# Gated one-hots on VectorE: one bf16 compare over eight tokens and wide fp32 multiplies in place of fused fp32 tensor_scalars

## The chip, the cores and the metric
The kernel runs on one core of a Trainium2 chip. The metric is the device time of one execution in microseconds; three timed runs of the kernel before gave a median of 1782.91 us (1781.59 to 1785.38 us). One further execution was recorded by the hardware profiler and is read below.

## The reference, cut to what matters
The program is one step of a decoder layer for 576 tokens (512 of a prompt, 64 of samples): windowed attention and a spatial gating unit in parallel, a merge, then a retrieval over 128 x 128 single-neuron experts (PEER), then a small per-layer gate. The change touches the retrieval alone. In the reference, for each token and each of 8 heads, 16 experts are chosen, and their outputs are added with a weight:

```
cand = (s_top[:, :, 0, :, None] + s_top[:, :, 1, None, :]).reshape(blk, PEER_HEADS, -1)
best, pos = lax.top_k(cand, PEER_TOPK)
idx = jnp.take_along_axis(cand_idx, pos, axis=-1)      # e0 * 128 + e1
gate = jax.nn.softmax(best, axis=-1)
act = jax.nn.gelu(jnp.einsum('thkd,td->thk', expert_u[idx], xb))
out = jnp.einsum('thkd,thk->td', expert_v[idx], gate * act)
```

A token thus has 128 chosen experts (8 heads x 16), each with a first index e0, a second index e1 and a gate.

## The kernel before, in words
The kernel computes the retrieval in two ways. For 192 tokens it gathers the chosen rows of the two expert tables from memory, one row per token by an indirect DMA on GpSimd's queue (line 707), and VectorE takes a dot product with each row (line 719) or adds it with its weight (line 726). For the other 384 tokens it computes all 16384 experts densely: stage 1 (function `stage1`, line 761 on) multiplies the tokens by 128 blocks of the first table, stage 2 (line 939) by 128 blocks of the second, and between the two the activations are multiplied by a gate plane (line 974) that is zero where an expert was not chosen.

Each weight block of either stage is loaded by SyncE's queue and split on the chip in two parts: ScalarE rounds it (w_hi, line 66) and VectorE subtracts (w_lo, line 67), and TensorE runs three products in place of one (line 82).

The gate planes are built by `build_g`, once for each of 24 groups of 16 tokens, in four steps of four tokens. For one token, the 128 chosen experts lie on the partitions. One one-hot matrix (128 x 128, expert by index) is made from e0, another from e1, one of the two carries the gate, and a matmul of the two (line 822) gives the 128 x 128 gate plane of the token. Transposed indices and gates for 128 tokens stand in a tile `ew` (columns: minus the gate, e1, the gate, e0), made by `make_ew` on ScalarE.

The four steps of a group alternate. In the even ones ScalarE makes the gated one-hot `oa` of e0, eight instructions for four tokens (lines 810 and 811), and VectorE the plain one-hot `ob` of e1, one compare of 512 elements a partition (line 813). In the odd ones VectorE makes both: the plain `oa` by one compare of 512 (line 816), and the gated `ob` by four instructions, each of which compares and multiplies one token's 128 elements (line 819). ScalarE then evicts the four planes to the tile `gs` (line 823), reading them across so that the four tokens lie side by side, and SyncE's queue writes `gs` to memory once per group.

The groups are not alone. The loop over `tb` runs some blocks of stage 1 ahead of each group up to a goal, the rest of the expert retrieval (lines 611 to 693) between the first groups, and `pay` lets a few gathers through per block and per group (none from group 22 on). VectorE therefore holds, in one queue, the one-hots, the splits of the weights, the retrieval and the dot products of the gathered rows; `rowp` has 5 row buffers, so GpSimd's next gather waits for VectorE. The order of the instructions on each engine is fixed before the run by the framework's scheduler, from priorities and its own estimates of cost.

Of the kernel before, what the change touches and what calls it, by code (L numbers as in the profile page):

```python
# [9 lines left out]
BF16 = mybir.dt.bfloat16  # L10
U32 = mybir.dt.uint32
AF = mybir.ActivationFunctionType
ALU = mybir.AluOpType
# [4 lines left out]
P = 128  # L18
# [6 lines left out]
TB = 16  # L25
# [3 lines left out]
SPILL = set(range(2, 40, 2))  # L29
NSP = len(SPILL)  # L30
GT = (2.0, 3.5)
ONE = (1, 2)
TAIL0 = 112
TAIL1 = 122
S1_TOPK = (4, 9, 13)
# [12 lines left out]
def tile_decoder_step(ctx: ExitStack, tc: tile.TileContext, a, o):  # L48
    nc = tc.nc
    V, A, T, G, S = nc.vector, nc.scalar, nc.tensor, nc.gpsimd, nc.sync  # L50

    def pool(stack, name, bufs, side="left", **kw):
        return stack.enter_context(tc.tile_pool(name=name, bufs=bufs, side=side, reuse_waits="tile", **kw))
# [6 lines left out]
    def cload(name, shape, pl=None):  # L60
        t = (pl or const).tile(shape, F32, name="c_" + name, bufs=1)
        S.dma_start(t, a[name])
        return t
# [62 lines left out]
    def bank(tag):  # L126
        return psB.tile([P, 512], F32, name=tag)
# [50 lines left out]
    for k in range(KC):  # L178
        with tc.high_priority(offset=500):
# [3 lines left out]
                               op0=ALU.mult, op1=ALU.subtract)  # L183
# [22 lines left out]
    iota = cload("iota", [P, P])  # L206
# [251 lines left out]
    for i in range(24):  # L458
        if i < 8:
            t, g = (svT, suT)[i // 4], i % 4  # L460
            z = t[:, g, :]
            w_chunk(6 + i, z, lambda cols: A.activation(z[:, cols], z[:, cols], AF.Gelu_apprx_tanh))
        else:
            c, br = divmod(i - 8, 2)
# [63 lines left out]
    for c0, r in tilesA:  # L528
# [4 lines left out]
        for hh in range(2):  # L533
            hs = slice(hh * 512, (hh + 1) * 512)
            pt = bank("pt")
            for k in range(4):
                x1k = x1[hh * 4 + k][:, c0:c0 + r]
                T.transpose(out=pt[:r, k * P:(k + 1) * P], in_=x1k, identity=ident)
                if r == NS:
# [3 lines left out]
                                   op0=ALU.mult, op1=ALU.mult)  # L543
# [186 lines left out]
    for i in range(16):  # L730
        h, c = i // 4 + i % 2 * 4, i // 2 % 2
# [14 lines left out]
    ewT = []  # L746
# [35 lines left out]
    def make_ew(e0, e1_, gtf):  # L782
        pt = bank("pt")
        for q, src in enumerate((e1_, gtf, e0)):
            T.transpose(out=pt[:, q * P:(q + 1) * P], in_=src, identity=ident)
        ew = ep.tile([P, 4, P], F32, name="ew")
        A.activation(ew[:, 1:4, :], pt[:, 0:3 * P].rearrange("p (a b) -> p a b", a=3), AF.Copy)
        A.activation(ew[:, 0, :], pt[:, P:2 * P], AF.Copy, scale=-1.0)
        ewT.append(ew)

    found = {}
    tqs.close()
# [1 line left out]
    gs_s = ExitStack()  # L794
    ep = pool(gs_s, "ep", 2)
    op = pool(gs_s, "op", 2)
    gsp = [pool(gs_s, "gsp%d" % i, 1) for i in range(2)]

    def build_g(tb):
        ti, t0 = divmod(tb * TB, P)  # L800
        ew = ewT[ti]
        gs = gsp[(tb + 1) % 2].tile([P, NJ, TB], F32, name="gs")
        for t4 in range(0, TB, 4):
            pt = psB.tile([P, 512], F32, name=("sc", "pt")[t4 // 4 % 2])
            oa = op.tile([P, 4, P], F32, name="oa")
            ob = op.tile([P, 4, P], F32, name="ob")
            c = t0 + t4
            if (tb * TB + t4) // 4 % ONE[1] < ONE[0]:
                for t in range(4):
                    A.activation(oa[:, t, :], iota, AF.Abs, scale=-1.0, bias=ew[:, 3, c + t:c + t + 1])  # L810
                    A.activation(oa[:, t, :], oa[:, t, :], AF.Relu, scale=ew[:, 0, c + t:c + t + 1],
                                 bias=ew[:, 2, c + t:c + t + 1])
                V.tensor_tensor(ob, iota[:, None, :].to_broadcast([P, 4, P]),
                                ew[:, 1, c:c + 4][:, :, None].to_broadcast([P, 4, P]), op=ALU.is_equal)
            else:
                V.tensor_tensor(oa, iota[:, None, :].to_broadcast([P, 4, P]),
                                ew[:, 3, c:c + 4][:, :, None].to_broadcast([P, 4, P]), op=ALU.is_equal)
                for t in range(4):
                    V.tensor_scalar(ob[:, t, :], iota, ew[:, 1, c + t:c + t + 1], ew[:, 2, c + t:c + t + 1],
                                    op0=ALU.is_equal, op1=ALU.mult)  # L820
            for t in range(4):
                T.matmul(pt[:, t * P:(t + 1) * P], lhsT=oa[:, t, :], rhs=ob[:, t, :], start=True, stop=True)  # L822
            A.activation(gs[:, :, t4:t4 + 4], pt.rearrange("p (t j) -> p j t", t=4), AF.Copy)
        if tb == NB // TB - 1:
            A.activation(g0, gs[:, 0:JB, :], AF.Copy)
        S.dma_start(gd[:, :, tb].rearrange("c p j t -> p c (j t)"), gs.rearrange("p (c j) t -> p c (j t)", j=JB))
# [11 lines left out]
    for tb in range(NB // TB):  # L838
        if tb == TBK:
            for i, r_ in enumerate(rest_t):  # L840
                for _ in r_:
                    pass
                make_ew(*found[5 - len(rest_t) + i])
            tks.close()
            late = pool(aLs, "aL", 1, "right")
            acp.append(late.tile([P, RING - NXP, NB], F32, name="aL"))
            g0 = late.tile([P, JB, TB], F32, name="g0")
        if tb < TBK:
            goal = S1_TOPK[2] + (tb + 1) * (S1_PRE - S1_TOPK[2]) // TBK
        else:  # L850
            goal = S1_PRE + (tb - TBK + 1) * (NSP + RING - 1 - S1_END - S1_PRE) // (NB // TB - TBK)
        while len(acts) < goal:
            stage1()
        if tb == 0:
            make_ew(*found[2])
        build_g(tb)
        for _ in range(2):
            if rest_t and next(rest_t[0], 1) == 1:
                rest_t.pop(0)
                make_ew(*found[4 - len(rest_t)])  # L860
        pay(GT[tb >= TBK] if tb < 22 else 0)
# [267 lines left out]
```

## Time and profile before
| | |
|---|---|
| median of three timed runs | 1782.91 us |
| profiled execution | 1776.88 us |
| its span, first to last instruction | 1775.1 us |
| TensorE, VectorE, ScalarE busy | 98%, 81%, 49% |
| stretch in which the gate planes are built | 605 to 882 us |
| granted TensorE clock, mean | 0.996 of full speed |

A busy TensorE is modelled from pipelined matmuls, so a busy share near full may still hide gaps; the pitch of undisturbed matmuls shows how many. The durations of VectorE's instructions overlap by some 0.08 us, so what one of them costs its queue is read from its start to the start of the next.

### The profile page before, as it was taken

To read this page: it belongs to the slowest core of one execution; us is meant where nothing else is said; L and a number is where in the kernel's file an instruction comes from. 1 tells how busy PE (TensorE), PEld (TensorE's weight loads), DVE (VectorE), ACT (ScalarE), POOL (GpSimd) and SP (SyncE) were. 2 spreads that over 40 slices of the span, in tenths; PEclk is the share of its full clock that TensorE was granted. 3 is DMA by queue.
4 is the path that set the end of the run, shared out by engine and by line. 5 is a ranking of instruction groups with operands and counts; after the bars stand their busy time and mean duration, and the time that the engine had idled before them with its cause. 6 is when DMAs were issued, how large, how long until landed. Compare 5 with 4: busy or idle time off the path is not lost.

```text
span 1775.1 us, 27763 instructions
## 1 busy us (share of the span) xinstructions
PE 1744.3 (98%) x10094; PEld 1575.1 (89%) x10094; DVE 1434.0 (81%) x2876; ACT 867.0 (49%) x1525; POOL 525.9 (30%) x390
## 2 busy tenths in 40 slices
PE   7999999999999899999999999999999999999998
PEld 7988999999999899999988887899899899887876
DVE  6455556548999999999898888998888888999862
ACT  6567444343236698999833333333333333333441
POOL 0000000000002112455245554454544554566300
PEclk9999999999999999999999999999999999999999
DMA  7211233443226577999999999999999999999741
GB/s 242 75 60 38 71 105 122 141 152 106 81 92 225 173 244 235 361 350 355 352 388 367 371 388 364 394 410 369 365 338 360 364 334 331 335 379 376 284 132 70
DMA packets 176457, 457.06 MB, mean 257 GB/s; under 512 B 15552, under 2 KB 76736, under 8 KB 174272
## 3 DMA queue, kind: packets, MB, share of 16 engines
q1 hardware_dynamic: 120736, 253.22, 40.6%
q0 software_dynamic: 55584, 202.07, 30.8%
q8 instruction: 79, 1.29, 0.3%
q14 instruction: 58, 0.48, 0.1%
HBM read 420.18 MB, written 35.78 MB: 257 GB/s over the span
## 4 chain that ended last, share of the span: by engine, by line
PE 77%; issue 7%; DVE 6%; DMA 5%; POOL 3%; ACT 1%; SPq 0%; DVEq 0%; POOLq 0%; ACTq 0%
PE mm L82 36%; PE oacc L939 21%; PE pv L82 5%; POOL row L707 3%; PE sc L822 2%; DMA row<-peer_v,idx 2%; PE pt L822 2%; PE oacc L902 2%; DVE w_lo L67 2%; PE sc L82 1%; DMA x1c<-ad 1%; DVE row L719 1%; DMA row<-peer_u,idx 1%; PE sc L580 1%; PE pv L447 1%
## 5 line engine op out<-in xcount | busy, mean ns | idle before, releaser
L66 ACT ACTIVATE w_hi<-w_raw 128x1024 fp32r<-128x1024 f32 x325 | 343.9, 1059 | 372.9 <-PE mm L82 287.1
L707 POOL DMA_INDIRECT row<-peer_u,idx x192 | 261.1, 1360 | 872.0 <-issue 520.8
L67 DVE TENSOR_TENSOR w_lo<-w_raw,w_hi 128x1024 fp32r<-128x1024 f32 x325 | 396.6, 1221 | 74.0 <-ACT w_hi L66 73.7
L82 PE MATMUL mm<-xd,w_hi 128*128 128x384 f32 x1552 | 405.9, 341 | 0.5 <-ACT w_hi L66 0.5
L82 PE MATMUL mm<-x,w_hi 128*128 128x256 f32 (+1 forms) x1600 | 329.7, 300 | 9.8 <-ACT x L181 9.5
L707 POOL DMA_INDIRECT row<-peer_v,idx x192 | 263.3, 1372 | 231.8 <-DVE acc L726 202.8
L82 PEld LDWEIGHTS mm<-xd,w_hi 128*128 128x128 f32 x1552 | 281.6, 189 | 5.9 <-ACT w_hi L66 0.8
L82 PEld LDWEIGHTS mm<-x,w_hi 128*128 128x128 f32 x1600 | 257.8, 190 | 24.1 <-ACT x L181 10.0
L82 PE MATMUL mm<-xd,w_lo 128*128 128x384 f32 x776 | 264.4, 341 | 3.7 <-DVE w_lo L67 3.7
L726 DVE SCALAR_TENSOR_TENSOR acc<-row,wts,acc 128x1024 f32<-128x1024 f32 x192 | 245.8, 1280 | 5.3 <-DMA row<-peer_v,idx 4.9
L939 PE MATMUL oacc<-w_hi,wl 128*128 128x512 f32 x768 | 242.0, 397 | 3.7 <-DVE wl L67 3.6
L939 PE MATMUL oacc<-w_lo,wh 128*128 128x512 f32 x768 | 242.0, 396 | 0.4 <-DVE w_lo L67 0.4
L939 PE MATMUL oacc<-w_hi,wh 128*128 128x512 f32 x768 | 242.3, 396 | 0.0
L719 DVE SCALAR_TENSOR_TENSOR row<-row,xr 128x1024 f32<-128x1024 f32 x192 | 231.6, 1221 | 11.0 <-DMA row<-peer_u,idx 8.6
L82 PE MATMUL mm<-x,w_lo 128*128 128x256 f32 (+1 forms) x800 | 236.6, 296 | 0.0
L939 PEld LDWEIGHTS oacc<-w_hi,wl 128*128 128x128 f32 x768 | 144.3, 188 | 39.6 <-DVE wl L67 5.5
L939 PEld LDWEIGHTS oacc<-w_lo,wh 128*128 128x128 f32 x768 | 144.4, 188 | 35.5 <-DVE w_lo L67 1.7
L939 PEld LDWEIGHTS oacc<-w_hi,wh 128*128 128x128 f32 x768 | 143.7, 188 | 29.4 <-ACT xr L921 0.8
L82 PEld LDWEIGHTS mm<-x,w_lo 128*128 128x128 f32 x800 | 151.7, 190 | 1.1 <-issue 0.8
L82 PEld LDWEIGHTS mm<-xd,w_lo 128*128 128x128 f32 x776 | 147.0, 189 | 4.7 <-DVE w_lo L67 4.7
L82 PE MATMUL pv<-xd,w_hi 128*128 128x384 f32 x496 | 136.7, 348 | 0.7 <-ACT x L776 0.7
L66 ACT ACTIVATE wh<-x 128x384 fp32r<-128x384 f32 x66 | 34.7, 526 | 162.6 <-PE oacc L939 153.1
(304 smaller groups left out, 2308.8 us busy)
## 6 DMA issues: line engine op xcount, KB each, us to landing
w_raw<-peer_uT SPq DMA_DIRECT2D x128, 512.0 KB
w_raw<-peer_v SPq DMA_DIRECT2D x128, 512.0 KB
gd<-gs SPq DMA_DIRECT2D x24, 1024.0 KB
gs<-gd SPq DMA_DIRECT2D x15, 1536.0 KB
w_raw<-w_in SPq DMA_DIRECT2D x30, 512.0 KB
w_raw<-peer_wq SPq DMA_DIRECT2D x16, 512.0 KB
w_raw<-w_br SPq DMA_DIRECT2D x8, 512.0 KB
w_raw<-w_out SPq DMA_DIRECT2D x8, 512.0 KB
```

What stands on the lines that cost most here:

```text
L66: A.activation(hi, src, AF.Copy)
L67: V.tensor_sub(lo, src, hi.bitcast(F32))
L82: mark_pe[0] = T.matmul(ps, lhsT=w[wi][:, wk + k, :], rhs=x[xi][k], start=i == 0, stop=i == n - 1)
L447: T.matmul(ps[:r], lhsT=xi[:, k, :r], rhs=wl_[k][wi][:, hh * 512:(hh + 1) * 512], start=i == 0, stop=i == 5)
L580: T.matmul(ps[:, b * P:(b + 1) * P], lhsT=qp[:, b * P:(b + 1) * P], rhs=sk, start=True, stop=True)
L707: ins = G.indirect_dma_start(out=row_, out_offset=None, in_=table, in_offset=bass.IndirectOffsetOnAxis(ap=ix, axis=0))
L719: V.scalar_tensor_tensor(row_, row_, 1.0, xrs[ti], op0=ALU.mult, op1=ALU.mult, accum_out=dots[:, s:s + 1])
L726: V.scalar_tensor_tensor(accs[ti], row_, wts[:, s:s + 1], accs[ti], op0=ALU.mult, op1=ALU.add)
L822: T.matmul(pt[:, t * P:(t + 1) * P], lhsT=oa[:, t, :], rhs=ob[:, t, :], start=True, stop=True)
L902: T.matmul(ps[hh][:r], lhsT=xi[:, k, :r], rhs=w[k][wi][:, hh * 512:(hh + 1) * 512], start=k == 0 and xi is xh and wi == 0, stop=k == KC - ...
L939: mark_pe[0] = T.matmul(oacc[t][hh], lhsT=wi[:, ts], rhs=vi[:, hh * 512:(hh + 1) * 512], start=j == 0 and last == 0 and vi is vh, stop=j = ...
```

## The change: what it does
The odd steps of a group change on VectorE. Before the four steps, one tensor_tensor compares, for the eight tokens of the two odd steps, a bf16 copy of the index ramp (`iota4`, each index repeated for four tokens, made once on ScalarE) with a bf16 copy of e1 (`ewh`, cast by ScalarE in `make_ew`). Its result `hot` is bf16 and holds, for each index, two runs of four tokens. In each odd step one tensor_tensor then multiplies `hot`, read so that the index runs innermost, by the fp32 gate and writes `ob` in fp32 as before. The four fused tensor_scalars of the step are gone. `hot` has one buffer; the new tiles lie in a pool of their own (`hp`). The even steps, `oa`, the matmuls and the evictions stay. The pattern that picked the odd steps (`ONE`) is written out and picks the same ones.

```
+        ewh = ep.tile([P, P], BF16, name="ewh")
+        A.activation(ewh, pt[:, 0:P], AF.Copy)
...
+    hp = pool(gs_s, "hp", 1)
+    iota4 = hp.tile([P, P, 4], BF16, name="iota4")
+    A.activation(iota4, iota[:, :, None].to_broadcast([P, P, 4]), AF.Copy)
...
+        hot = hp.tile([P, P, 2, 4], BF16, name="hot")
+        e1c = ewh[:, t0:t0 + TB].rearrange("p (g s t) -> p g s t", g=2, s=2)[:, :, 1, :]
+        V.tensor_tensor(hot, iota4[:, :, None, :].to_broadcast([P, P, 2, 4]),
+                        e1c[:, None].to_broadcast([P, P, 2, 4]), op=ALU.is_equal)
...
-                for t in range(4):
-                    V.tensor_scalar(ob[:, t, :], iota, ew[:, 1, c + t:c + t + 1], ew[:, 2, c + t:c + t + 1],
-                                    op0=ALU.is_equal, op1=ALU.mult)
+                V.tensor_tensor(ob, hot[:, :, t4 // 8, :].rearrange("p x t -> p t x"),
+                                ew[:, 2, c:c + 4][:, :, None].to_broadcast([P, 4, P]), op=ALU.mult)
```

## Rows read from the trace of the kernel before

**Rows 1.** Engine totals of the page: busy us, share of the span, instructions.
```profile
PE 1744.3 (98%) x10094; PEld 1575.1 (89%) x10094; DVE 1434.0 (81%) x2876; ACT 867.0 (49%) x1525; POOL 525.9 (30%) x390
```

**Rows 2.** Busy time of each engine by stretch: us, busy (instructions), clock, DMA.
```profile
605.00:720.00 115.00, 112.63 (x722) 108.47 (x723) 113.44 (x308) 104.67 (x227) 24.10 (x17) 0.99 0.77 240
720.00:840.00 120.00, 119.85 (x800) 114.80 (x799) 119.05 (x236) 111.97 (x270) 61.06 (x41) 1.00 1.04 358
840.00:882.00 42.00, 42.00 (x280) 39.88 (x279) 34.87 (x63) 38.11 (x92) 11.16 (x9) 1.00 0.99 353
...
882.00:1140.00 258.00, 251.31 (x1189) 216.15 (x1188) 228.85 (x297) 89.34 (x121) 128.31 (x92) 1.00 0.98 379
```

**Rows 3.** Chain of waits: 605 to 720 and 720 to 840 us by line; two pieces.
```profile
by line: PE pv L82 29.6%; PE mm L82 21.8%; PE pt L822 12.2%; PE sc L822 12.0%; DVE row L719 3.1%; DVE w_lo L67 3.0%; DVE ob L819 2.6%; issue 1.9%; DVE oa L816 1.6%; ACT sp L632 1.6%; DVE c L625 1.3%; DVE pos L627 1.2%; PE pt L785 1.2%; DVE 
by line: PE pv L82 31.6%; PE mm L82 30.2%; PE sc L822 19.0%; PE pt L822 17.9%; issue 0.7%; DVE ob L813 0.5%; DVE row L719 0.1%; DVEq L67 0.0%
...
737.96 0.90 PE pt L822 x8
...
753.33 4.16 PE mm L82 x24
```

**Rows 4.** The same stretches, of one line's instructions: L82, L822, then VectorE's L813.
```profile
720.00:840.00 120.00, 91.44 (x435) 73.86 (x436) 1.00 1.04 358
...
720.00:840.00 120.00, 53.82 (x365) 47.44 (x363) 1.00 1.04 358
...
605.00:720.00 115.00, 12.35 (x18) 0.99 0.77 240
720.00:840.00 120.00, 15.21 (x23) 1.00 1.04 358
840.00:882.00 42.00, 5.46 (x8) 1.00 0.99 353
```

**Rows 5.** Waits of TensorE's weight loads, 605 to 882 us: total, times, longest.
```profile
PEld sc L822 <- ACT oa L811: 4.6, 17, 1.0
PEld pt L785 <- DVE e L658: 3.6, 1, 3.6
...
PEld pt L822 <- DVE ob L819: 0.2, 1, 0.2
```

**Rows 6.** Groups of VectorE instructions, 605 to 882 us: count, busy us, mean ns.
```profile
L819 DVE TENSOR_SCALAR ob<-c_iota,ew 128x128 f32<-128x128 f32 x192 | 55.2, 349 | 0.1
L67 DVE TENSOR_TENSOR w_lo<-w_raw,w_hi 128x1024 fp32r<-128x1024 f32 x43 | 52.5, 1222 | 4.7 <-ACT w_hi L66 4.6
...
L813 DVE TENSOR_TENSOR ob<-c_iota,ew 128x512 f32<-128x512 f32 x48 | 33.0, 688 | 2.1 <-PE sc L822 1.1 <-PE pt L822 0.8
...
L653 DVE TENSOR_TENSOR l<-pr 128x1024 bf16<-128x1024 bf16 x6 | 4.1, 690 | 0.0
```

**Rows 7.** VectorE in order of time: start us, us, instruction.
```profile
639.70 0.70 DVE L653 TENSOR_TENSOR l<-pr 128x1024 bf16<-128x1024 bf16 x1
640.30 0.22 DVE L682 RECIPROCAL den<-den 128x8 f32<-128x8 f32 x1
...
734.86 1.22 DVE L67 TENSOR_TENSOR w_lo<-w_raw,w_hi 128x1024 fp32r<-128x1024 f32 x1
735.99 0.69 DVE L813 TENSOR_TENSOR ob<-c_iota,ew 128x512 f32<-128x512 f32 x1
736.60 0.69 DVE L816 TENSOR_TENSOR oa<-c_iota,ew 128x512 f32<-128x512 f32 x1
737.20 1.11 DVE L819 TENSOR_SCALAR ob<-c_iota,ew 128x128 f32<-128x128 f32 x4
738.23 0.68 DVE L813 TENSOR_TENSOR ob<-c_iota,ew 128x512 f32<-128x512 f32 x1
```

**Rows 8.** Groups of ScalarE's evictions of 512 elements: count, busy us, mean ns.
```profile
L823 ACT ACTIVATE gs<-pt 128x512 f32<-128x512 f32 x48 | 28.2, 587 | 1.2 <-PE pt L822 0.9
...
L451 ACT ACTIVATE st<-pv 128x512 f32<-128x512 f32 x8 | 4.7, 588 | 6.7 <-PE pv L447 6.7
```

More of the change, by code (lines that the diff above doesn't have):

```diff
@@ L31 @@
 GT = (2.0, 3.5)
-ONE = (1, 2)
 TAIL0 = 112
@@ L786, in make_ew @@
         ew = ep.tile([P, 4, P], F32, name="ew")
+        ewh = ep.tile([P, P], BF16, name="ewh")
+        A.activation(ewh, pt[:, 0:P], AF.Copy)
         A.activation(ew[:, 1:4, :], pt[:, 0:3 * P].rearrange("p (a b) -> p a b", a=3), AF.Copy)
         A.activation(ew[:, 0, :], pt[:, P:2 * P], AF.Copy, scale=-1.0)
-        ewT.append(ew)
+        ewT.append((ew, ewh))
     found = {}
@@ L797, in tile_decoder_step @@
     gsp = [pool(gs_s, "gsp%d" % i, 1) for i in range(2)]
+    hp = pool(gs_s, "hp", 1)
+    iota4 = hp.tile([P, P, 4], BF16, name="iota4")
+    A.activation(iota4, iota[:, :, None].to_broadcast([P, P, 4]), AF.Copy)
     def build_g(tb):
         ti, t0 = divmod(tb * TB, P)
-        ew = ewT[ti]
+        ew, ewh = ewT[ti]
+        hot = hp.tile([P, P, 2, 4], BF16, name="hot")
+        e1c = ewh[:, t0:t0 + TB].rearrange("p (g s t) -> p g s t", g=2, s=2)[:, :, 1, :]
+        V.tensor_tensor(hot, iota4[:, :, None, :].to_broadcast([P, P, 2, 4]),
+                        e1c[:, None].to_broadcast([P, P, 2, 4]), op=ALU.is_equal)
         gs = gsp[(tb + 1) % 2].tile([P, NJ, TB], F32, name="gs")
@@ L807, in build_g @@
             c = t0 + t4
-            if (tb * TB + t4) // 4 % ONE[1] < ONE[0]:
+            if t4 // 4 % 2 == 0:
                 for t in range(4):
```

## The prediction
> **What bounds the kernel now.** I read the page's engine totals first [rows 1]: TensorE is busy 1744.3 us of a span of 1775.1 us, VectorE 1434.0 us. The totals say "TensorE", but they average over stages, and the change lives in one stage only, the building of the gate planes from 605 to 882 us. So the second view is the table by stretches of that stage [rows 2]. In it three engines are nearly full at once: from 605 to 720 us TensorE is busy 112.63 and VectorE 113.44 of 115 us, from 720 to 840 us 119.85 and 119.05 of 120 us, and ScalarE 104.67 and 111.97 us. Only from 840 to 882 us, where no gathers are paid for any more, does VectorE have room (34.87 of 42 us).
>
> Two full engines don't tell which one paces. The chain of waits does [rows 3]: from 605 to 720 us VectorE's rows (row L719, w_lo L67, ob L819, oa L816, c L625, pos L627) hold 3.1 + 3.0 + 2.6 + 1.6 + 1.3 + 1.2 = 12.8% of it beside TensorE; from 720 to 840 us the chain is TensorE for 98.7% and VectorE's ob for 0.5%. A busy TensorE is modelled, so I check it by its pitch: 24 matmuls of 384 columns run in 4.16 us when nothing holds them (0.173 us each) and 8 of the fp32 gate matmuls in 0.90 us (0.1125 us each) [rows 3]. With the counts of 720 to 840 us [rows 4] that is 435 x 0.173 + 365 x 0.1125 = 75.3 + 41.1 = 116.4 of 120 us: TensorE can win at most 3.6 us there, whatever VectorE does. What it does wait for in the stage is mostly not the changed code: 4.6 us for ScalarE's oa (L811), 3.6 us for the retrieval's e (L658) [rows 5].
>
> **The change part by part.** Durations overlap from one VectorE instruction to the next, so I price by the slot, from one start to the next start [rows 6, 7].
> Removed, in each group of 16 tokens: two sets of four tensor_scalars. Their rows say 349 ns each, but a set that starts at 737.20 lets the next instruction start at 738.23: 1.03 us a set, 2.06 us a group.
> Added, per group: one bf16 compare of 1024 elements a partition, and two multiplies of 512 elements.
> The compare: all three operands are bf16, and the innermost run in each is four tokens. The retrieval's bf16 tensor_tensor of the same size (L653) takes 690 ns, where the fp32 subtraction of 1024 takes 1222 ns [rows 6]; one that starts at 639.70 is followed at 640.30, a slot of 0.60 us [rows 7]. From above it is bounded by the slot of the fp32 form, 734.86 to 735.99, 1.13 us. I take 0.60, since L653 has the same types and halves down to short runs.
> The multiplies: 512 elements, fp32 gate, fp32 result, so the nearest row is the fp32 compare of 512 (L813, 688 ns), slot 735.99 to 736.60, 0.61 us. That is the lower end. But their first operand is read across: the four-token block is turned, so neighbouring elements of the inner run lie eight bf16, 16 bytes, apart. No VectorE row reads like that. The upper end is the slot of a pass twice as long, 1.13 us for 1024 elements. The nearest row for reading across is ScalarE's eviction of the gate planes, which picks its inner four elements 512 bytes apart and takes 587 ns, against 588 ns for a straight eviction of 512 elements (L451) [rows 8]: no loss. It is another engine and another memory, but it is the only access of this kind in the trace, and I take 0.61 and keep 1.13.
> Sum: 2.06 - (0.60 + 2 x 0.61) = 0.24 us less of VectorE per group, 5.8 us for 24 groups.
>
> The Trainium skill speaks against the multiplies. "SBUF — State Buffer" (Door 1, the note on cachelines) has 16-byte lines and wants at least two hits on a line for full rate; an inner step of 16 bytes hits each line once. The same note counts eight bf16 as a free stride, so it can be read both ways; the trace has no VectorE row to decide. By the strict reading the sum would be that of the first rival below.
>
> What of 5.8 us reaches the end? The compares on line 813 begin 18 times before 720 us, two a group, so 9 groups lie in the stretch where VectorE is on the chain, 23 starts or 11.5 groups lie in 720 to 840 us, and 4 groups behind it [rows 4]. In the first stretch 9 x 0.24 = 2.2 us can move the chain; as TensorE holds most of that chain too, I take 2.0. In 720 to 840 us the saving (2.8 us) becomes VectorE idle time behind a TensorE that paces, and in 840 to 882 us it joins the idle time that is there.
> Moved: the compare stands ahead of a group's first ob. It waits for the last multiply of the group before (one buffer), on the same engine, so nothing new is waited for; what queues behind it is the group's first ob for 0.60 us, inside a VectorE queue that gets shorter on the whole. In a VectorE-gated group the first gate matmul now waits for a whole multiply (0.61 us) where it waited for one tensor_scalar, and the fourth stops waiting 0.4 us earlier; TensorE issues them in a row of four and has other matmuls between, so I cost it at nothing. Should that cover fail, it is at most 0.35 us x 48 groups of four = 17 us, but TensorE waited for ob L819 for 0.2 us in the whole stage [rows 5], and so I don't count it.
> ScalarE gets three casts of 128 elements and one fill of 512, each no larger than what takes 0.59 us in rows 8, so under 2.4 us together. The fill and the first cast come before the first group; the other two casts stand ahead of evictions that a later group needs, and these casts are the only part on ScalarE's path, under 1.2 us in a stage in which it has 22 us free [rows 2]. No DMA is added or moved. Behind 882 us nothing is touched; the DMA share there is 0.98 [rows 2], and a start earlier by 2 us may be given back in part, which the range holds.
>
> So the profiled execution, 1776.88 us (its span and 1.78 us around it), would be 1774.9. The median of the three timed runs is 1782.91, 6.0 us above the profiled one; on that scale I forecast 1780.9 us. A change of 0.2%, 3.6 us, is about what a measurement of this kernel can tell from none, and the forecast lies inside.
>
> **Rivals.**
> 1. The turned read costs double, slower. If each multiply holds VectorE for 1.13 us, a group gains 2 x 0.52 - 0.24 = 0.80 us. VectorE has 1.6 us free in 605 to 720 and 1.0 us in 720 to 840 us: 9 x 0.80 - 1.6 = 5.6, and 11.5 x 0.80 - 1.0 = 8.2, while the last four groups fit in the idle 7 us. Together +13.8, 1796.7 us. It decides from the point where a multiply's slot exceeds about 0.79 us (two multiplies then eat the saving and the idle 2.6 us over 20.5 groups). For it: no VectorE row shows a read across, and VectorE has no room to hide one. Against it: ScalarE's turned read at full rate [rows 8]. The Trainium skill's note on cachelines, in its strict reading, is for it.
> 2. VectorE paces all the way to 840 us. Then 20.5 x 0.24 = 4.9 us come off, 1778.0 us. For it: VectorE is busy 119.05 of 120 us and the gathers wait for its rows; against it: the chain's 98.7% of TensorE.
> 3. The bf16 compare doesn't run at the fast rate with runs of four and repeated operands: 1.13 us instead of 0.60, +0.29 us a group, 9 x 0.29 - 1.6 = 1.0 and 11.5 x 0.29 - 1.0 = 2.3, so +3.3, 1786.2 us. Against it: L653's 690 ns.
> 4. It does nothing: the order of the instructions is written anew around other costs and the 2 us are lost in TensorE's gaps or to the DMA behind 882 us, 1782.9 us.
>
> **How the numbers follow.** Forecast 0.36, rival 1 0.28, rival 2 0.20, rival 3 0.08, rival 4 0.08. The likeliest case alone reaches from 1777 to 1784. Rival 1 is too likely to be left out, so the range goes from 1776 to 1797, which cuts off half of rival 1's spread and the best of rival 2. Faster by over 0.2%: most of rival 2 and a quarter of the forecast, 0.29. Slower: nearly all of rival 1, half of rival 3 and a bit of 4, 0.34. Within 0.2%: 0.37.
>
> **What would show it.** The multiply's mean in the list of groups: near 0.69 us is my forecast, near 1.22 us is rival 1. The compare near 0.69 us, or 1.22 us for rival 3. VectorE's busy time from 720 us to the end of the stage should drop by some 4 us with the stage no shorter (forecast) or shorter by as much (rival 2). ScalarE's oa should stay TensorE's main wait. I am wrong if the stage moves by over 4 us while the multiplies run at 0.69 us, or if the time moves behind 882 us.

## The result and the profile after

The changed kernel takes 1792.51 us (median of six runs, 1789.3 to 1798.18) beside 1781.89 us for the kernel before on the same chip: 10.6 us more, a ratio of 1.0064 with a 95% interval of 1.0048 to 1.0079. The forecast was 1780.9 us and 2 us faster, so its sign was wrong. The recorded execution has a span of 1787.5 us, 12.4 us more than before. Single executions differ by some us, so the timed difference (8.6 to 14.1 us by its interval) and that of the two spans agree. Rival 1 is what happened: the multiply that reads the one-hot turned is slow.

The groups of VectorE instructions of the kernel after, between 605 and 890 us (count, busy us, mean ns), answer to [rows 6]:

```profile
L826 DVE TENSOR_TENSOR ob<-hot,ew 128x512 f32<-128x512 bf16 x48 | 51.4, 1070 | 0.0
...
L821 DVE TENSOR_TENSOR ob<-c_iota,ew 128x512 f32<-128x512 f32 x48 | 32.7, 682 | 3.0 <-PE pt L829 1.7 <-PE sc L829 1.3
L808 DVE TENSOR_TENSOR hot<-iota,ewh 128x1024 bf16<-128x1024 bf16 x24 | 16.4, 683 | 0.0
```

The bf16 compare (L808) takes 683 ns as priced. The multiply (L826) has as many elements as the plain compare of 512 (L821, 682 ns) and takes 1070 ns. In order of time, VectorE after, against [rows 7]:

```profile
801.66 0.69 DVE L808 TENSOR_TENSOR hot<-iota,ewh 128x1024 bf16<-128x1024 bf16 x1
802.27 0.69 DVE L821 TENSOR_TENSOR ob<-c_iota,ew 128x512 f32<-128x512 f32 x1
...
804.64 1.08 DVE L826 TENSOR_TENSOR ob<-hot,ew 128x512 f32<-128x512 bf16 x1
805.64 0.68 DVE L821 TENSOR_TENSOR ob<-c_iota,ew 128x512 f32<-128x512 f32 x1
...
807.99 1.07 DVE L826 TENSOR_TENSOR ob<-hot,ew 128x512 f32<-128x512 bf16 x1
808.97 1.22 DVE L718 SCALAR_TENSOR_TENSOR row<-row,xr 128x1024 f32<-128x1024 f32 x1
```

The compare's slot is 0.61 us, the multiply's 1.00 and 0.98 us. A group of 16 tokens now costs 0.60 + 2 x 0.99 = 2.58 us where the removed instructions cost 2.06 us: 0.52 us more, 12.5 us in 24 groups. The stretches of the stage after (columns as in [rows 2]) show where they went:

```profile
605.00:720.00 115.00, 109.20 (x692) 103.13 (x691) 114.18 (x257) 103.11 (x223) 24.56 (x17) 0.99 0.73 231
720.00:840.00 120.00, 116.76 (x762) 108.83 (x760) 120.00 (x174) 108.49 (x259) 52.56 (x39) 1.00 1.02 345
840.00:882.00 42.00, 40.82 (x268) 38.38 (x268) 38.83 (x49) 37.67 (x93) 15.82 (x10) 1.00 0.97 337
```

From 720 to 840 us VectorE is busy 120.00 of 120 us, and TensorE, which had been busy 119.85, now 116.76 us with 762 matmuls in place of 800. VectorE has become the pacer there, and the waits of TensorE after (matmuls, then weight loads, 605 to 887 us: total, times, longest) name the instruction, where [rows 5] had ScalarE's oa in front and 0.2 us for the gated ob:

```profile
PE pt L829 <- DVE ob L826: 5.7, 21, 0.5
...
PEld pt L829 <- issue: 10.3, 19, 0.8
PEld pt L829 <- DVE ob L826: 4.5, 10, 0.7
PEld sc L829 <- ACT oa L819: 3.5, 12, 0.9
```

The largest of them, 10.3 us of weight loads under "issue", has no cause that the profile shows; the same line had 1.1 us in e1_straight_read below.

In the chain of waits from 605 to 720 us, VectorE's w_lo, ob and row stand in front, behind 22.3% of time without a shown cause, where [rows 3] had TensorE's pv and mm.

```profile
by line: issue 22.3%; DVE w_lo L66 10.1%; DVE ob L826 9.4%; DVE row L718 9.0%; POOL row L706 8.2%; PE pv L81 6.7%; DVE ob L821 4.5%; DVE oa L824 4.3%; DVE l L652 3.8%; DVE pr L646 3.0%; DVE c L624 2.0%; DVE pos L627 1.8%; DVE pos L626 1.8%;
```

From 720 to 840 us the chain names only GpSimd's gathers (34.7%) and time without a cause (67.7%), so it does not decide there. That VectorE paces rests on its 120.00 of 120 us and on e1_straight_read.

How much later is the stage? The last store of a gate plane is issued at 886.77 us, after 878.43 us before: 8.3 us. That mark alone misleads, since the two programs order their work differently. From 604 us to it TensorE has done 1000 block matmuls (those of the weight blocks, line 82 before and 81 after) in the kernel before and 976 after. The row counts TensorE's instructions of that line alone:

```profile
604.00:886.77 282.77, 206.69 (x976) 166.73 (x977) 0.99 0.89 297
```

The 24 that are missing are 24 x 0.173 = 4.2 us of work left for later, and 8.3 + 4.2 = 12.5 us. A mark with equal work in front is the first matmul that adds x1 (the retrieval's input, which is added to its result) into the accumulators in stage 2: in each kernel for which it is used below, 1488 block matmuls from 604 us on and all 64 weighted rows of the first gathered tile lie ahead of it. It comes at 1139.8 us before and at 1152.3 us after, again 12.5 us. From it to the end both kernels take the same time (635.3 and 635.2 us). That three ways of counting give 12.5 is in part luck: the first block matmul already starts at 513.5 us before and at 512.0 us after, so marks are good to some 2 us.

### The profile page after: what moved, and what is told of

Its sections match the earlier page's. It is cut to its first block, busy times and chain, and to the rows that moved or that the text cites. A ratio compares the mean times of both kernels' runs of the same rounds, so it can differ in the third digit from the quotient of the medians.

```text
span 1787.5 us, 27659 instructions
## 1 busy us (share of the span) xinstructions
PE 1747.7 (98%) x10094; PEld 1574.1 (88%) x10094; DVE 1444.5 (81%) x2756; ACT 870.4 (49%) x1529; POOL 524.9 (29%) x390
## 4 chain that ended last, share of the span: by engine, by line
PE 65%; issue 13%; DVE 8%; POOL 7%; DMA 5%; ACT 1%; POOLq 0%; SPq 0%; DVEq 0%; ACTq 0%
PE mm L81 32%; PE oacc L946 21%; POOL row L706 7%; DMA row<-peer_v,idx 2%; PE oacc L909 2%; DVE w_lo L66 2%; PE sc L81 1%; PE pv L81 1%; DVE row L718 1%; DMA x1c<-ad 1%; DMA row<-peer_u,idx 1%; PE sc L579 1%; PE pv L446 1%; PE pv L314 1%; PE sc L296 1%
## 5 line engine op out<-in xcount | busy, mean ns | idle before, releaser
L706 POOL DMA_INDIRECT row<-peer_u,idx x192 | 254.5, 1326 | 883.4 <-issue 516.1
L81 PE MATMUL mm<-x,w_hi 128*128 128x256 f32 (+1 forms) x1600 | 327.8, 298 | 10.6 <-ACT x L180 9.2
L706 POOL DMA_INDIRECT row<-peer_v,idx x192 | 268.9, 1400 | 233.7 <-DVE acc L725 205.0
L718 DVE SCALAR_TENSOR_TENSOR row<-row,xr 128x1024 f32<-128x1024 f32 x192 | 232.0, 1218 | 11.5 <-DMA row<-peer_u,idx 11.2
L65 ACT ACTIVATE wh<-x 128x384 fp32r<-128x384 f32 x66 | 34.7, 526 | 162.9 <-PE oacc L946 155.7
## 6 DMA issues: line engine op xcount, KB each, us to landing
w_raw<-peer_uT SPq DMA_DIRECT2D x128, 512.0 KB, 6.3
w_raw<-peer_v SPq DMA_DIRECT2D x128, 512.0 KB, 6.8
w_raw<-w_in SPq DMA_DIRECT2D x30, 512.0 KB, 3.4
w_raw<-peer_wq SPq DMA_DIRECT2D x16, 512.0 KB, 3.4
w_raw<-w_br SPq DMA_DIRECT2D x8, 512.0 KB, 3.6
w_raw<-w_out SPq DMA_DIRECT2D x8, 512.0 KB, 3.3
```

The costliest lines, as they stand in the source:

```text
L65: A.activation(hi, src, AF.Copy)
L81: mark_pe[0] = T.matmul(ps, lhsT=w[wi][:, wk + k, :], rhs=x[xi][k], start=i == 0, stop=i == n - 1)
L706: ins = G.indirect_dma_start(out=row_, out_offset=None, in_=table, in_offset=bass.IndirectOffsetOnAxis(ap=ix, axis=0))
L718: V.scalar_tensor_tensor(row_, row_, 1.0, xrs[ti], op0=ALU.mult, op1=ALU.mult, accum_out=dots[:, s:s + 1])
```

## The experiments

Theory: the read at a step of 16 bytes is what is slow, and VectorE has no room for it. Rival A: mixing a bf16 with an fp32 operand is slow. Rival B: the new order of instructions costs the time, not VectorE. Each ratio is to the kernel before on the same chip (medians 1778.66 to 1779.6 us).

**e1_straight_read.**
```
-                V.tensor_tensor(ob, hot[:, :, t4 // 8, :].rearrange("p x t -> p t x"),
+                V.tensor_tensor(ob, hot.rearrange("p (s t x) g u -> p s t (x g u)", s=2, t=4)[:, t4 // 8],
```


> The changed kernel with the multiply reading the same 512 elements of the one-hot tile in a row instead of turned (so the gated one-hots carry the matches of other tokens; the gate planes are not the reference's). Same instructions, types and sizes. Theory (the turned read at a step of 16 bytes is what is slow): the multiply falls from 1.07 to 0.69 us, VectorE's slots per group are 1.82 us against 2.06 before, the last gate-plane store is issued near 878 us as before, and the time is that of the kernel before or up to 3 us less (ratio 0.998 to 1.001). Rival A (a bf16 operand beside an fp32 one is what is slow): the multiply stays at 1.07 us and the time 10 us above before. Rival B (not VectorE's load but the new order of instructions and the new waits of the first gate matmul cost the time): the multiply falls to 0.69 us, but the time stays 8 to 11 us above before.

Measured: 1779.4 us, ratio 0.9995 (0.9980 to 1.0009). The multiply's group in this kernel:
```profile
L826 DVE TENSOR_TENSOR ob<-hot,ew 128x512 f32<-128x512 bf16 x48 | 32.8, 682 | 0.0
```
It falls from 1070 to 682 ns with the same types, so rival A falls. The order of the instructions on all five engines is the same, line for line, as in the changed kernel, so rival B falls too: 48 x (0.99 - 0.605) = 18.5 us of VectorE, and nothing else, part two programs whose ratios to the kernel before are 0.9995 and 1.0064. TensorE's waits for ob L826 are gone from the list of its waits but for 0.3 us of a weight load. But the 5.8 us less VectorE than before bring no gain that can be told from none. Of the 18.5 us between these two programs of one order, some 12 us reach the end.

**e2_step8.** The two blocks of four tokens stand apart, so the turned read steps by 8 bytes.
```
-        hot = hp.tile([P, P, 2, 4], BF16, name="hot")
+        hot = hp.tile([P, 2, P, 4], BF16, name="hot")
-        V.tensor_tensor(hot, iota4[:, :, None, :].to_broadcast([P, P, 2, 4]),
-                        e1c[:, None].to_broadcast([P, P, 2, 4]), op=ALU.is_equal)
+        V.tensor_tensor(hot, iota4[:, None].to_broadcast([P, 2, P, 4]),
+                        e1c[:, :, None, :].to_broadcast([P, 2, P, 4]), op=ALU.is_equal)
-                V.tensor_tensor(ob, hot[:, :, t4 // 8, :].rearrange("p x t -> p t x"),
+                V.tensor_tensor(ob, hot[:, t4 // 8].rearrange("p x t -> p t x"),
```


> The changed kernel with the eight tokens in two blocks of four, so that the multiply reads at a step of 8 bytes (two elements of each 16-byte stretch in a row) instead of 16; the compare stays one instruction of 1024. Theory in its line form (one read per 16 bytes is slow, two are not): multiply 0.69 us, as e1_straight_read, ratio to before 0.998 to 1.001. Theory in a smooth form (the cost grows with the step): a multiply between 0.75 and 0.95 us, VectorE's group 1.95 to 2.3 us, ratio 1.000 to 1.004. Rival A (mixed types): 1.07 us and ratio 1.006.

Measured: 1778.85 us, ratio 0.9994 (0.9979 to 1.0008).
```profile
L826 DVE TENSOR_TENSOR ob<-hot,ew 128x512 f32<-128x512 bf16 x48 | 32.7, 682 | 0.0
```
Two elements in each 16 bytes read in turn are enough for the full rate; the line form of the theory holds at this step. The order of instructions is again that of the changed kernel. So the change as meant, with every term of my sum as priced, is worth nothing measurable here.

**e3_steps.** Seven layouts in turn in the odd steps; the core of three of them:
```
+                if kind == 0:
+                    hot = hp.tile([P, P, 4], BF16, name="hot")
+                    V.tensor_tensor(hot, iota4, e1h[:, None, :].to_broadcast([P, P, 4]), op=ALU.is_equal)
+                    V.tensor_tensor(ob, hot.rearrange("p x t -> p t x"), gate4, op=ALU.mult)
+                elif kind == 1:
+                    hot = hp.tile([P, P, 6], BF16, name="hot")
...
+                elif kind == 4:
+                    hot = hp.tile([P, P, 4], F32, name="hot")
...
```


> One look for the price of the read alone. The odd steps rotate through seven layouts of the one-hot of four tokens, each with its own compare and then a multiply of 512 by the fp32 gate: bf16 at steps of 2 (straight), 8, 12, 16 and 32 bytes (the last in two halves of 256), fp32 at 8 and 16 bytes. Theory, line form: 0.69 us up to 8 bytes in either type, about 0.8 to 0.9 at 12, 1.07 us at 16 in either type and no more at 32 (two halves of 0.6 us). Rival A (mixed types): all bf16 forms 1.07 us, both fp32 forms 0.69 us. A third reading, that the number of elements counts and not the bytes (eight elements free or not): bf16 at 16 bytes and fp32 at 16 bytes would differ. The time of the whole says little.

The groups of the seven multiplies (in this order: 32 bytes in halves, fp32 at 16, bf16 at 16, bf16 at 12, fp32 at 8, bf16 at 8, bf16 straight):
```profile
L841 DVE TENSOR_TENSOR ob<-hot,ew 128x256 f32<-128x256 bf16 x14 | 9.2, 654 | 0.1
L846 DVE TENSOR_TENSOR ob<-hot,ew 128x512 f32<-128x512 f32 x7 | 7.6, 1082 | 0.0
L836 DVE TENSOR_TENSOR ob<-hot,ew 128x512 f32<-128x512 bf16 x7 | 7.5, 1069 | 0.0
L832 DVE TENSOR_TENSOR ob<-hot,ew 128x512 f32<-128x512 bf16 x7 | 5.9, 836 | 0.0
...
L852 DVE TENSOR_TENSOR ob<-hot,ew 128x512 f32<-128x512 f32 x7 | 4.8, 683 | 0.0
...
L828 DVE TENSOR_TENSOR ob<-hot,ew 128x512 f32<-128x512 bf16 x7 | 4.8, 682 | 0.0
L859 DVE TENSOR_TENSOR ob<-hot,ew 128x512 f32<-128x512 bf16 x6 | 4.1, 683 | 0.0
```
Bytes decide, not the type and not the number of elements: at 16 bytes 1069 ns in bf16 and 1082 in fp32, at 8 bytes 682 and 683. As an estimate, with the fixed part of a pass taken from 512 and 1024 elements in [rows 6] ((1222 - 688) / 512 = 1.04 ns an element, 154 ns fixed), an element costs 1.04 ns up to 8 bytes, (836 - 154) / 512 = 1.33 at 12, (1069 - 154) / 512 = 1.79 at 16 and (654 - 154) / 256 = 1.95 at 32. The last is a little dearer than I expected. The whole was timed once, 1790.78 us, and says little, as expected.

**e4_load_only.**
```
+        spare = hp.tile([P, 4, 108], F32, name="spare")
+        V.tensor_tensor(spare, iota[:, None, :108].to_broadcast([P, 4, 108]),
+                        ew[:, 3, t0:t0 + 4][:, :, None].to_broadcast([P, 4, 108]), op=ALU.is_equal)
```


> The kernel before with one spare compare of 432 fp32 elements per group on VectorE, ahead of the group's steps, whose result nobody reads: 0.53 us more VectorE per group (the slot of 512 less 80 elements), 12.6 us in 24 groups, about what the turned multiplies add (2 x 0.99 + 0.60 - 2.06 = 0.52 us per group). No turned read, no bf16. Theory (VectorE's load in a stage where it has no room is the whole price): the last gate-plane store comes 7 to 10 us later and the time is 8 to 12 us above before (ratio 1.005 to 1.007). Rival B (order and waits of the change): within 3 us of before. Rival C (TensorE or ScalarE pace the stage and take such a load in): within 3 us too.

Measured: 1797.93 us, ratio 1.0099 (1.0076 to 1.0121), so 17 us and more for 12.6 us of load: the direction is the theory's, the size is beyond the 8 to 12 us that I expected. The last store comes 16.4 us later, but the scheduler had put 56 more block matmuls and 4 more weighted rows ahead of it; at the x1 mark, with equal work, it is 1157.4 us, 17.6 late. Some 5 us come on top of the load. The new order of instructions may be the reason, but that was not tried; it limits what this run says to "a load on VectorE costs at least itself".

**e5_no_gate.** What would any saving on VectorE bring?
```
-                for t in range(4):
-                    V.tensor_scalar(ob[:, t, :], iota, ew[:, 1, c + t:c + t + 1], ew[:, 2, c + t:c + t + 1],
-                                    op0=ALU.is_equal, op1=ALU.mult)
+                V.tensor_tensor(ob, iota[:, None, :].to_broadcast([P, 4, P]),
+                                ew[:, 1, c:c + 4][:, :, None].to_broadcast([P, 4, P]), op=ALU.is_equal)
```


> The kernel before with the gate left out of the odd steps: the four tensor_scalars become one plain compare of 512, as in the even steps (half of the tokens' gate planes are then ungated, not the reference's). VectorE is 2 x (1.03 - 0.61) = 0.84 us lighter per group, 20 us over 24 groups. It asks what any saving on VectorE can bring here. Theory (TensorE is within 7 us of full over the stage, and what is won there is given back to the DMA behind it): the last gate-plane store comes 3 to 8 us earlier than 878 us, the time is no more than 4 us below before (ratio 0.998 to 1.000). Rival 2 of the prediction (VectorE paces the stage): the store 12 us or more earlier and the time 8 to 15 us below before (ratio 0.992 to 0.995).

Measured: 1776.78 us, ratio 0.9990 (0.9977 to 1.0003). The last store comes at 861.96 us, 16.5 us earlier and not the 3 to 8 that the theory expected, which looked like rival 2 of the prediction; but 913 block matmuls lie ahead of it in place of 1000, and 87 x 0.173 = 15.1 us of the 16.5 are only work put behind. At the x1 mark the kernel is where it was, 1140.7 us. From 604 us to that mark (columns as in [rows 2]; the kernel before had TensorE 525.59, VectorE 497.01 of 535.80 us and a DMA share of 0.95):
```profile
604.00:1140.70 536.70, 527.20 (x2985) 482.58 (x2986) 477.74 (x764) 343.32 (x707) 212.63 (x158) 0.99 0.94 342
```
VectorE is 19 us less busy and the stretch is not shorter. TensorE's own pitch does not fill it either: 1488 x 0.173 + 768 x 0.1125 is 344 us, and the 720 matmuls of stage 2 ahead of the mark add 720 x 4.20 / 18 = 168 us (a set of 18 takes 4.20 us on the kernel before's chain), 512 of 537 us. Of what this row lists, the DMA stays, and a wait points at it: from 880 to 1140 us VectorE stands 14.7 us before the landing of spilled activations that are read back (x1c) in the kernel before, and 19.8 us here. The half-row runs below put it to the test.

**e6_step8_more_gathers and e7_before_more_gathers.** Both with
```
-G2 = (1.6, 2.0)
+G2 = (1.55, 2.0)
-GT = (2.0, 3.5)
+GT = (2.2, 3.8)
```
on top of e2_step8 and of the kernel before.

> e2_step8 with the VectorE time it saves filled by gathers: GT from (2.0, 3.5) to (2.2, 3.8) lets about six more rows through during the gate planes (6 x 1.14 = 6.8 us of VectorE against the 5.8 us saved), and G2 from 1.6 to 1.55 lets as many fewer through behind them, where the DMA share is 0.98. Theory (behind the stage the DMA limits): the stretch from the last gate-plane store to the first add of x1 shrinks by 2 to 5 us, the stage stays as before, and the time is 2 to 4 us below before (ratio 0.998 to 0.999). Rival (TensorE limits there as well, or six rows are too few to matter): ratio 0.999 to 1.001.

> The control for e6_step8_more_gathers: the kernel before with the same GT and G2. VectorE has no room for six more rows (6.8 us), so by the theory the stage ends 3 to 7 us later and the time is 1 to 5 us above before (ratio 1.000 to 1.003). If it is as good as e6_step8_more_gathers, the lighter one-hots are worth nothing even with the gathers moved.

Measured: 1782.57 us, ratio 1.0023 (1.0012 to 1.0034), and 1787.51 us, ratio 1.0049 (1.0032 to 1.0066). The expected gain did not come: more gathers in the stage cost time in both. But the kernel with the lighter multiplies is 4.9 us faster than the other, near the 5.8 us that these save. From 840 to 882 us VectorE is busy 41.59 of 42 us in e7_before_more_gathers and 35.46 in e6_step8_more_gathers, where the kernel before had 34.87 [rows 2]. So where VectorE is filled up, the saving seems to be worth its price.

**e8_half_rows, e9_half_rows_no_gate, e10_half_rows_step8.** On the kernel before, on e5_no_gate and on e2_step8:
```
-        ins = G.indirect_dma_start(out=row_, out_offset=None, in_=table,
+        ins = G.indirect_dma_start(out=row_[:, 0:512], out_offset=None,
+                                   in_=table.rearrange("r (h d) -> (r h) d", h=2),
...
+                                       row_[:, None, 0:512].to_broadcast([P, 2, 512]), 1.0,
```


> The kernel before with each gathered row cut to half (2 KB in place of 4 KB; VectorE reads the half twice, so its 1024 elements per row stay; the gathered tokens' results are not the reference's). About 100 MB of 457 MB less DMA. The base of the next two. Theory (behind the gate planes, from 880 to 1140 us, DMA sets the pace): the DMA share there falls from 0.98 to 0.75 or less and the kernel is 5 to 20 us faster than before (ratio 0.989 to 0.997). Rival (VectorE's or TensorE's own work fills that stretch): within 3 us of before.

> e5_no_gate with the rows cut to half in the same way: what 20 us less VectorE in the gate-plane stage bring where the DMA behind it has room. Theory (e5_no_gate lost its 16 us of stage to the DMA behind it): the time is 8 to 16 us below e8_half_rows. Rival (it lost them to something else, as VectorE's queue or TensorE): within 3 us of e8_half_rows, as e5_no_gate was within 3 us of before.

> e2_step8 with the rows cut to half in the same way: the change as it was meant (0.24 us less VectorE per group, 5.8 us in all) where the DMA behind has room. Theory: 2 to 5 us below e8_half_rows. Rival: within 1 us of it.

Measured: 1774.75, 1765.66 and 1767.56 us; ratios 0.9977 (0.9968 to 0.9987), 0.9928 (0.9916 to 0.9940) and 0.9934 (0.9922 to 0.9946). The stretch behind the gate planes in e8_half_rows, and then in e9_half_rows_no_gate, against 251.31 us of TensorE and a DMA share of 0.98 in [rows 2]:
```profile
882.00:1140.00 258.00, 258.00 (x1242) 225.02 (x1241) 237.75 (x308) 92.38 (x125) 154.81 (x96) 1.00 0.82 293
```
```profile
882.00:1140.00 258.00, 258.00 (x1246) 225.50 (x1245) 237.84 (x309) 92.12 (x123) 150.25 (x98) 1.00 0.80 285
```
The base gains 4 us only, less than the 5 to 20 that I expected, and the DMA share falls to 0.82 where I expected 0.75 or less. TensorE, which idled 6.7 of these 258 us in the kernel before, is now busy all of them, so the rival (TensorE's own work fills that stretch) is right in part. But on this base the lighter VectorE pays: 9.1 us for leaving the gate out (nothing measurable with whole rows) and 7.2 us for the one-hots at a step of 8 bytes (0.24 us a group, 5.8 us by their slots; the recorded spans are 4.6 us apart). So with whole rows, as far as these runs show, it is the DMA that hides most of what a lighter VectorE saves. The order of the instructions differs between these kernels too, and e4_load_only left 5 us unexplained, so the direction is surer than the sizes. Which transfer decides was not taken apart further.

**e11_step8_later_gathers and e12_before_later_gathers.** A try to relieve the DMA ahead of the x1 mark, on e2_step8 and on the kernel before:
```
-GP = [0.5, 0.0, 1.65]
+GP = [0.5, 0.0, 1.5]
-G2 = (1.6, 2.0)
+G2 = (1.6, 2.25)
```


> e2_step8 with some gathers behind the gate planes put off: GP's third value from 1.65 to 1.5 and G2 from (1.6, 2.0) to (1.6, 2.25), so that about one row in twenty moves from the stretch of 880 to 1520 us to the one behind it, where the DMA share is 0.88. About 4 rows (2 MB, 5 us of DMA at 379 GB/s) leave 880 to 1140 us. Theory (that stretch is paced by DMA and eats the 4 us that e2_step8 wins in the stage): 2 to 5 us below before (ratio 0.997 to 0.999). Rival (the stretch behind pays for it, VectorE being busy 157 of 174 us from 1526 to 1700 us): no gain or a loss (ratio 0.999 to 1.003).

> The control for e11_step8_later_gathers: the kernel before with the same GP and G2. Theory: it gains less, 0 to 3 us (ratio 0.998 to 1.000), since it reaches the stretch 4 us later; e11_step8_later_gathers is 1 to 4 us faster than it. Rival: both the same.

Measured: 1783.5 us, ratio 1.0024 (1.0015 to 1.0033), and 1785.05 us, ratio 1.0028 (1.0018 to 1.0038). Both miss, and the stated rival fits: from the x1 mark to the end they take 638.4 and 641.2 us, the kernel before 635.3, so the rows that were put off are paid for behind. VectorE is busy 165.93 and 164.64 of the 174 us from 1526 to 1700 us in them, 157.20 in the kernel before. The control also reaches the x1 mark 4.5 us late (1144.3 us), which stays unexplained, and the intervals of the two overlap, so no difference between them is shown. No version that still computes the reference was found measurably faster than the kernel before.

The marks and loads side by side (VectorE busy and DMA share from 604 us to the x1 mark). They are single recorded executions, whose first block matmul starts anywhere between 512.0 and 515.4 us, so differences of 3 us between marks mean little; e1_straight_read was recorded in an execution 2.2 us above its median.

| kernel | last store | x1 mark | VectorE busy | DMA share | timed ratio |
|---|---|---|---|---|---|
| before | 878.43 | 1139.8 | 497.01 | 0.95 | 1 |
| after | 886.77 | 1152.3 | 506.70 | 0.93 | 1.0064 |
| e1_straight_read | 875.81 | 1144.6 | 492.42 | 0.94 | 0.9995 |
| e2_step8 | 874.65 | 1141.4 | 490.55 | 0.94 | 0.9994 |
| e4_load_only | 894.79 | 1157.4 | 510.77 | 0.93 | 1.0099 |
| e5_no_gate | 861.96 | 1140.7 | 477.74 | 0.94 | 0.9990 |
| e8_half_rows | 875.97 | 1135.3 | 499.21 | 0.80 | 0.9977 |
| e9_half_rows_no_gate | 861.01 | 1128.3 | 481.56 | 0.81 | 0.9928 |
| e10_half_rows_step8 | 873.27 | 1130.7 | 493.78 | 0.81 | 0.9934 |

## Why the prediction was wrong

- **The step that failed** is the price of the multiply: "The nearest row for reading across is ScalarE's eviction of the gate planes ... no loss. It is another engine and another memory, but it is the only access of this kind in the trace, and I take 0.61 and keep 1.13." The slot is 0.99 us. The row I took was near by its kind of access and far by its engine and its memory, and it shows nothing of VectorE: with the same order of instructions, 0.61 against 0.99 us is the whole difference between e1_straight_read and the changed kernel.
- **The rule I weighed** came out in its strict reading. The Trainium skill ("SBUF — State Buffer", Door 1, the note on cachelines) wants two hits on each 16-byte line, and the runs agree: 682 ns at 8 bytes, 1069 at 16, and 836 at 12, where some lines are hit twice. Its sentence that a stride of eight bf16 is free does not hold here: a step of eight bf16 is the one that costs 1.7 times as much an element (1.79 against 1.04 ns).
- **Rival 1** had the mechanism and the side, but its price of 1.13 us was an end, not the value; 0.99 us gives 0.52 us a group. Its formula would then give 9 x 0.52 - 1.6 + 11.5 x 0.52 - 1.0 = 8.1 us. The timed medians grew by 10.6 us (8.6 to 14.1), the recorded span by 12.4 us, and 24 x 0.52 = 12.5 us. The formula let idle time and the room of the last four groups take 4.4 us of that, and little or nothing of this shows: from 604 us to the last store VectorE's idle time is 7.1 us before (274.43 - 267.34) and 7.0 us after (282.77 - 275.79). The measured time lies in the stated range only because that was widened for this rival.
- **The compare** (0.60 us forecast, 0.61 measured) and the saving of 0.24 us a group at a straight read were right, as e1_straight_read and e2_step8 show; rival 3 falls.
- **The 2.0 us that were to reach the end** can't be told from nothing: e1_straight_read and e2_step8 are at 0.9995 and 0.9994, with intervals of some 0.15% to either side. I had put the limit on TensorE ("TensorE can win at most 3.6 us there"). e5_no_gate and the half-row runs point to another one: up to the x1 mark, at a DMA share of 0.94 to 0.95, what VectorE saves does not show, and with half the row data it appears. I had let the DMA take back "in part" what is won before it; nothing measurable is left. Rival 2 falls with whole rows.
- **The first gate matmul waiting for a whole multiply**, costed at nothing, is right at 0.61 us a multiply (0.3 us of waits in e1_straight_read) and wrong at 0.99 us (5.7 us of waits before matmuls and 4.5 us before weight loads in the kernel after). ScalarE's three casts take 0.28 us each, and e1_straight_read and e2_step8, which have them, lose nothing that can be measured.

## What to carry to other kernels

Before a layout is chosen for the writer of a tile, price the reader: on VectorE two elements in each 16 bytes kept the full rate here, one did not, and the same tile in two blocks cured it without another instruction. A price taken from another engine's row is no bound; where both signs hang on it, that access is the one thing to measure first. And where several engines and the DMA are near full at once, a saving on one of them may bring nothing while a loss on it comes through nearly whole; compare stages at a mark with equal work in front, not at the last instruction of a kind.

## What the runs showed of the hardware that I had not expected

The cost of VectorE's turned read is graded, not a switch: 1.04 ns an element up to a step of 8 bytes, 1.33 at 12, 1.79 at 16, 1.95 at 32, the same for bf16 and fp32 at equal bytes (1069 and 1082 ns at 16, 682 and 683 ns at 8). It is not the doubling that I kept as the upper end. ScalarE's eviction in the same kernel reads its inner elements 512 bytes apart in the accumulators at no loss (587 ns against 588 ns straight, [rows 8]), so the one access can't stand for the other. Whether the engine or the memory makes the difference, no run here shows.
